# Attention scores of two tiles in one step, grouped by kind of matmul, and one ring of four PSUM banks for scores and transposes

## The chip, the cores and the metric

One core of one Trainium2 chip runs the whole program. The metric is the device time of one execution in microseconds, lower is better. TensorE (PE) does the matmuls, VectorE (DVE) and ScalarE (ACT) the elementwise work, SyncE (SP) issues most transfers, GpSimd (POOL) does little.

## The reference

One layer of an encoder, 2048 tokens of width 1024, on a grid of 32 rows by 64 columns. After an adaptive layer norm one input projection feeds two branches: a gated linear recurrence in both directions (HGRN, 8 heads of 128) and a neighbourhood attention (16 heads of 64, a window of 8 rows by 16 columns, clamped at the grid's edge, with a bias table). Both are gated, concatenated, projected by `w_out`, added to the input and normalised. The change touches the attention alone:

```
# _neighbourhood_attention, per grid row r, queries in 4 blocks of 16 columns, keys of 32 columns per block
s = jnp.einsum('bhjqd,bhrjcd->bhjqrc', q_row, k_blk).astype(jnp.float32) * scale
bias = jnp.take(col_bias, row_off, axis=1).transpose(0, 2, 3, 1, 4)
s = jnp.where(col_mask[:, :, None, :], s + bias[None], -jnp.inf)
p = jax.nn.softmax(s.reshape(B, H, nqb, NA_KC, KR * NA_SPAN), axis=-1)
o = jnp.einsum('bhjqrc,bhrjcd->bhjqd', p, v_blk)
...
y_na = o_na * jax.nn.silu(g_n)
```

## The kernel before, in words

**Stages.** The start and the first half of the attention (to about 560 us, with 8 head pairs over the first 8 grid rows), the recurrence (to about 1779 us), the second half of the attention (1779 to 2392 us, 8 head pairs over the other 24 rows), the output projection. A head pair is `w` in the first half, `u` in the second.

**A tile** is one block of 128 queries (8 grid rows, called a row group R, by 16 columns, number j) of two heads. A head pair has 4 tiles (R = 0) in the first half and 12 (R = 1, 2, 3 with j = 0 to 3) in the second. Keys of a tile are `nr` rows of 32 columns: 352, 480 or 384 in all. For one tile:

- `scores` has PE make two score banks (one per head): a product with the rounded keys, all 128 partitions high (KA and KB, L981), and added onto it one with the small remainder of the keys, 64 partitions high (KL, L984; "half-height"). The rounding is that of the fp32r type.
- Softmax, per head: DVE adds the bias, negates and takes the minimum (`shifted`, L993), ACT exponentiates and sums (`powers`, L998), DVE takes the reciprocal (L1002) and multiplies (`shares`, L1003).
- `turned` has PE transpose the shares in blocks of 128 (L1025) into PSUM; DVE and ACT copy them to SBUF (L1029, L1031).
- `sums` multiplies them with the values (L1044): per tile 16 matmuls of 128 columns by 64 (12 for R = 3). When a row group's four tiles are done, DVE multiplies by the gate into `yv` (L1054).

**The step.** `natten_woven` goes through the tiles one at a time. Step i issues the scores of tile i, then the sums of tile i-2, then hands over to the dense matmuls, then the transposes of tile i-1 (`turn(pipe, 2)`), then dense matmuls again, and then the tasks listed for step i.

**Dense matmuls** (L259, `pj`) are the projections of the next head pair's queries, keys, values and gates, three per group and eight groups per result in the second half; `weave` issues them between the pieces of a step. Each `yield x` of the step says how much: total / steps times x, in units of 0.68 per group. In the second half `steps` is 24 with two yields of 1 for each of the 12 tiles, which makes about six matmuls at each yield. Weights are split into a rounded part and a remainder by ACT and DVE (`wh`, `wl`, L758, L759).

**Tasks** prepare what comes next (`prep_now`, `prep_next`): `k` splits a piece of the next head pair's keys (rounded part on ACT, L922; remainder on DVE, L924), `q` the queries (L907, L908 on ACT, L909, L910 on DVE), `gate` makes the gate (L937, L317, L318, L319, L939), `table` loads a bias table, `v` the values. In the second half there is one set of KA, KB and KL: keys of the next head pair are written, piece by piece, over rows that this head pair's later tiles no longer read, and a piece waits for the matmuls that read it last. In the first half there are two sets.

**The order.** The program fixes PE's order by hand (as the code is written); DVE's, ACT's and SP's order within the attention comes from a scheduler, in which the softmax and the copies have priority (`tc.high_priority`). Each engine runs its instructions in the order given.

**PSUM.** The attention's eight banks: two for scores (`sc`), two for transposes (`pt`), two for sums (`po`), and two outside this table for dense results.

## Time and profile before

| | us |
|---|---|
| median of three runs | 2708.0 |
| lowest and highest run | 2706.22 and 2708.6 |
| span of the profiled execution | 2706.9 |
| second half of the attention | 1779 to 2392 |
| one head pair of it (five alike) | 67.1 |

The profile is of one execution, and its span is the profiled execution's own time. How to read it: the first line of the page gives each engine's busy time, its share of the span and its number of instructions (x). PE is TensorE's matmuls, PEld its weight loads, which run beside them. In rows of the timeline the columns are start in us, duration, engine, line of the kernel, operation, output <- inputs by the program's names, partitions x elements, number of instructions in the row (x), and in square brackets the idle time of the engine before it with what ended it. A pipelined matmul's duration is longer than the distance to the next one's start, so distances of starts are what PE spends. In group rows the numbers behind the bar are busy us in total, mean ns of one, and the idle time ahead of them. In rows of windows, each engine's busy time is followed by the number of its instructions, then the granted TensorE clock (1.00 is full), the DMA engines' share and GB/s.

### The profile page before, as it was taken

To read this page: it belongs to the slowest core of one execution; us is meant where nothing else is said; L and a number is where in the kernel's file an instruction comes from. 1 tells how busy PE (TensorE), PEld (TensorE's weight loads), DVE (VectorE), ACT (ScalarE), POOL (GpSimd) and SP (SyncE) were. 2 spreads that over 40 slices of the span, in tenths; PEclk is the share of its full clock that TensorE was granted. 3 is DMA by queue.
4 is the path that set the end of the run, shared out by engine and by line. 5 is a ranking of instruction groups with operands and counts; after the bars stand their busy time and mean duration, and the time that the engine had idled before them with its cause. 6 is when DMAs were issued, how large, how long until landed. Compare 5 with 4: busy or idle time off the path is not lost.

```text
span 2706.9 us, 46031 instructions
## 1 busy us (share of the span) xinstructions
PE 2612.5 (97%) x17328; PEld 2156.8 (80%) x17328; DVE 1766.4 (65%) x4351; ACT 1425.5 (53%) x2808; POOL 105.3 (4%) x142
## 2 busy tenths in 40 slices
PE   4999999989999999999999999989999999899998
PEld 3888888878888888888888888887777776678887
DVE  5445445477777778878777786455777777648443
ACT  4534444366666666666666666344666666431110
POOL 0000000000000000000000000000000000032221
PEclk8999999999999999999999999999999999999999
DMA  6566454212111126212222112354445445344331
GB/s 240 153 189 161 126 171 148 103 50 75 63 63 63 59 75 223 82 36 75 75 75 75 63 61 94 100 158 124 122 126 130 126 132 137 105 138 139 98 93 55
DMA packets 226559, 296.45 MB, mean 110 GB/s; under 512 B 28456, under 2 KB 117288, under 8 KB 226217
## 3 DMA queue, kind: packets, MB, share of 16 engines
q1 hardware_dynamic: 226337, 293.52, 35.3%
q8 instruction: 136, 2.23, 0.3%
q14 instruction: 86, 0.70, 0.1%
HBM read 218.24 MB, written 66.99 MB: 105 GB/s over the span
## 4 chain that ended last, share of the span: by engine, by line
PE 71%; DMA 2%; DVE 2%; ACT 1%; SPq 1%; issue 0%; DVEq 0%; ACTq 0%
PE pj L259 38%; PE ps L1384 4%; PE ps L1385 4%; PE ps L1386 4%; PE ps L1044 3%; PE ps L1025 3%; PE pj L272 2%; PE ps L458 2%; PE ps L450 1%; PE ps L981 1%; PE ps L984 1%; PE ps L525 1%; PE ps L497 1%; PE ps L549 1%; PE ps L551 1%; PE ps L623 1%
## 5 line engine op out<-in xcount | busy, mean ns | idle before, releaser
L259 PE MATMUL pj<-h,wh 128*128 128x512 f32 x4016 | 1289.1, 402 | 11.4 <-ACT h L224 6.2
L259 PEld LDWEIGHTS pj<-h,wh 128*128 128x128 f32 x4016 | 727.9, 189 | 173.3 <-issue 21.3
L259 PE MATMUL pj<-h,wl 128*128 128x512 f32 x2008 | 788.6, 393 | 0.1
L259 PEld LDWEIGHTS pj<-h,wl 128*128 128x128 f32 x2008 | 378.2, 188 | 83.2 <-DVE wl L759 0.5
L998 ACT ACTIVATE pbuf<-pbuf,mx 128x480 f32<-128x480 f32 (+2 forms) x256 | 164.3, 643 | 174.8 <-DVE mx L993 174.0
L993 DVE CUSTOM_DVE_ANT_1 pbuf<-ps,bias 128x480 f32<-128x480 f32 (+2 forms) x256 | 144.0, 595 | 134.9 <-PE ps L984 121.4
L272 PE MATMUL pj<-wh,h 128*128 128x256 f32 x1024 | 195.7, 288 | 0.3 <-ACT e L732 0.3
L272 PEld LDWEIGHTS pj<-wh,h 128*128 128x128 f32 x1024 | 163.6, 193 | 4.2 <-issue 2.5
L249 ACT ACTIVATE wh<-wr 128x512 fp32r<-128x512 f32 x192 | 120.2, 626 | 82.2 <-PE pj L259 69.3
L250 DVE TENSOR_TENSOR wl<-wr,wh 128x512 fp32r<-128x512 f32 x192 | 131.7, 686 | 46.6 <-ACT wh L249 45.6
L272 PE MATMUL pj<-wl,h 128*128 128x256 f32 x512 | 145.6, 284 | 0.0
L1031 ACT ACTIVATE pt<-ps 128x512 f32<-128x512 f32 (+1 forms) x128 | 69.1, 540 | 132.3 <-PE ps L1025 132.0
L1029 DVE COPY pt<-ps 128x512 f32<-128x512 f32 (+1 forms) x128 | 79.3, 619 | 84.2 <-PE ps L1025 83.2
L1044 PE MATMUL ps<-pt,V 128*64 128x128 f32 x1408 | 108.3, 285 | 16.1 <-ACT pt L1031 7.8
L444 DVE TENSOR_TENSOR de<-e,de 128x512 f32<-128x512 f32 x64 | 44.3, 692 | 118.9 <-ACT de L443 118.9
L1025 PE MATMUL ps<-ident,pbuf 128*128 128x128 f32 x896 | 119.2, 273 | 1.5 <-DVE pbuf L1003 1.5
L1025 PEld LDWEIGHTS ps<-ident,pbuf 128*128 128x128 f32 x896 | 105.6, 141 | 17.4 <-issue 2.3
L1044 PEld LDWEIGHTS ps<-pt,V 128*64 128x64 f32 x1408 | 76.1, 138 | 44.5 <-issue 20.7
L1003 DVE TENSOR_SCALAR pbuf<-pbuf,mx 128x480 f32<-128x480 f32 (+2 forms) x256 | 108.2, 437 | 5.1
L1360 ACT ACTIVATE yh<-yr 128x512 fp32r<-128x512 f32 x52 | 32.7, 629 | 130.9 <-PE ps L1385 113.9
L1433 DVE TENSOR_TENSOR vt<-ps,gt 128x512 f32<-128x512 f32 x24 | 16.5, 692 | 127.6 <-PE ps L1386 127.6
L272 PEld LDWEIGHTS pj<-wl,h 128*128 128x128 f32 x512 | 99.0, 193 | 0.8 <-issue 0.5
(266 smaller groups left out, 4634.3 us busy)
## 6 DMA issues: line engine op xcount, KB each, us to landing
wr<-in_w_in SPq DMA_DIRECT2D x276, 256.0 KB
V<-nv SPq DMA_DIRECT2D x256, 64.0 KB
yr<-yq SPq DMA_DIRECT2D x64, 256.0 KB
bias<-tint SPq DMA_DIRECT2D x24, 480.0 KB
x<-in_x SPq DMA_DIRECT2D x32, 256.0 KB
ada<-in_ada_w SPq DMA_DIRECT2D x16, 512.0 KB
wr<-in_w_v SPq DMA_DIRECT2D x32, 256.0 KB
nv<-vt SPq DMA_DIRECT2D x32, 256.0 KB
```

The source lines that it names most:

```text
L249: act.activation(hi, raw, AF.Copy)
L250: dve.tensor_tensor(lo, raw, hi, op=ALU.subtract)
L259: pe.matmul(pz, a, b, start=(k == 0 and n == 0), stop=(k == KT - 1 and n == 2))
L272: pe.matmul(pzs[tp][:, i * 256:(i + 1) * 256], a, b, start=(k == 0 and n == 0 and i == 0), stop=(k == KT - 1 and n == 2), skip_group_check ...
L993: return dve.tensor_tensor_reduce(s[:, 0:nk].rearrange("p (r c) -> p r c", c=32), sc[:, 0:nk].rearrange("p (r c) -> p r c", c=32), bt[:, 0 ...
L998: act.activation(s[:, 0:nk], s[:, 0:nk], AF.Exp, scale=-1.0, bias=mx[:, 0:1], accum_out=mx[:, 1:2])
L1003: dve.tensor_scalar(s[:, 0:nk], s[:, 0:nk], mx[:, 2:3], 1.0, op0=ALU.mult, op1=ALU.mult)
L1025: pe.transpose(ptp[:, c * P:(c + 1) * P], s[:, c * P:(c + 1) * P], ident)
L1044: pe.matmul(self.po[R][hs_, j * P:(j + 1) * P], self.st.V[c0 + c][:, j * P + hh * 64:j * P + hh * 64 + 64], pts[hh][:, c * P:(c + 1) * P], ...
L1384: pe.matmul(pz, yh[:, kk], wh, start=first, stop=False)
L1385: pe.matmul(pz, yh[:, kk], wl, start=False, stop=False)
L1386: pe.matmul(pz, yl[:, kk], wh, start=False, stop=last)
```

## The change

`scores` takes two tiles of one row group at once. It issues their four key matmuls, then their four half-height ones; the softmax is a method of its own and is called once for each tile. A step of `natten_woven` now covers two tiles: scores of both, `sums` of both tiles of the step before (32 matmuls in a block, 24 for R = 3), dense matmuls (0.8), transposes of this step's first tile, dense matmuls (1.8), transposes of this step's second tile, tasks of the first, dense matmuls (1.4), tasks of the second. So the transposes of a tile come in the step of its scores; before, they came one step (one tile) later. `turn` is gone. Score and transpose banks are one ring of four (`sp`) instead of two and two; the start keeps two and two in its own PSUM phase (`SPS`). The last head pair of the first half spreads its dense matmuls over 8 instead of 10. The computed values are the same.

```diff
-        def scores(self, R, j):
+        def scores(self, R, js):
+
             k0, nr = TILE[R]
-            bt = self.st.table(KIND[R], j)
             nk = nr * 32
-            scs = [ps("sc"), ps("sc")]
-            qs = [z[:, j * P:(j + 1) * P] for z in self.st.Q[R]]
             keys = keysets[self.p % len(keysets)]
...
-            for hh in range(2):
-                pe.matmul(scs[hh][:, 0:nk], qs[hh], kv(("KA", "KB")[hh]), start=True, stop=False, skip_group_check=True)
-            for hh in range(2):
-                hs_ = slice(hh * 64, hh * 64 + 64)
-                pe.matmul(scs[hh][:, 0:nk], qs[hh][hs_], kv("KL")[hs_], start=False, stop=True, skip_group_check=True)
+            for j in js:
+                bt = self.st.table(KIND[R], j)
+                scs = [ps("sc"), ps("sc")]
+                qs = [z[:, j * P:(j + 1) * P] for z in self.st.Q[R]]
+                tiles.append((j, bt, scs, qs))
+                for hh in range(2):
+                    pe.matmul(scs[hh][:, 0:nk], qs[hh], kv(("KA", "KB")[hh], j), start=True, stop=False, skip_group_check=True)
+            for j, bt, scs, qs in tiles:
+                for hh in range(2):
+                    hs_ = slice(hh * 64, hh * 64 + 64)
+                    pe.matmul(scs[hh][:, 0:nk], qs[hh][hs_], kv("KL", j)[hs_], start=False, stop=True, skip_group_check=True)
+            return [self.softmax(nr, bt, scs) for j, bt, scs, qs in tiles]
...
-        for i, (R, j) in enumerate(n.order):
-            pipe.append([n, R, j, n.scores(R, j)])
-            if len(pipe) > 2:
-                m, r, c, pts = pipe.pop(0)
-                m.sums(r, c, pts)
-            yield 1
-            turn(pipe, 2)
-            yield 1
+
+        def tasks(i):
             for f, *a in now.get(i, []) + later.get(i, []) + extra.get(i, []):
                 f(*a)
+
+        for i in range(0, len(n.order), 2):
+            R, js = n.order[i][0], [j for _, j in n.order[i:i + 2]]
+            ss = n.scores(R, js)
+            sums(pipe)
+            yield 0.8
+            p0 = n.turned(R, ss[0])
+            yield 1.8
+            p1 = n.turned(R, ss[1])
+            tasks(i)
+            pipe += [(n, R, js[0], p0), (n, R, js[1], p1)]
+            yield 1.4
+            tasks(i + 1)
...
-    NPS = {"sc": 2, "pt": 2, "po": 2}
+    SPS = {"sc": 2, "pt": 2, "po": 2}
+    NPS = ({"sp": 4, "po": 2}, {"sc": "sp", "pt": "sp"})
...
-                nxt, dense, total, steps = None, hgrn_dense(0, 0, feed=feed), HTOT, 10
+                nxt, dense, total, steps = None, hgrn_dense(0, 0, feed=feed), HTOT, 8
...
-    with psum_phase("n1", NPS), phase("n1", NB1, SM1), tc.manual_schedule(engines={mybir.EngineType.PE}):
+    with psum_phase("n1", *NPS), phase("n1", NB1, SM1), tc.manual_schedule(engines={mybir.EngineType.PE}):
```

Two places of the order show the change. The first is PE in the second half, head pair u = 2, at the last two tiles of R = 2. Before, the last tile but one: scores, sums of the tile two before it, six dense matmuls, then transposes of the tile before it (`pbuf` numbers name the shares' buffers; the sums' and dense matmuls' further rows are left out).

```order
L981 MATMUL ps_21145<-KA_3552_18657,Q_20498 128x480
L981 MATMUL ps_21146<-KB_3553_18658,Q_20499 128x480
L984 MATMUL ps_21145<-KL_3554_18659,Q_20498 128x480
L984 MATMUL ps_21146<-KL_3554_18659,Q_20499 128x480
L1044 MATMUL ps_21161<-pt_21121,V_20432 64x128
...
L259 MATMUL pj_21135<-h_10754,wh_20915 128x512
...
L1025 MATMUL ps_21184<-ident,pbuf_18651 128x128 x4
L1025 MATMUL ps_21191<-ident,pbuf_18653 128x128 x4
```

Now, the pair: both tiles' keys, both tiles' half-heights, 32 sums (the first is shown), three dense matmuls, and transposes of the pair's own first tile.

```order
L985 MATMUL ps_21163<-KA_3552_18661,Q_20516 128x480
L985 MATMUL ps_21164<-KB_3553_18662,Q_20517 128x480
L985 MATMUL ps_21167<-KA_3552_18661,Q_20516 128x480
L985 MATMUL ps_21168<-KB_3553_18662,Q_20517 128x480
L989 MATMUL ps_21163<-KL_3554_18663,Q_20516 128x480
...
L1053 MATMUL ps_21195<-pt_21094,V_20491 64x128
...
L259 MATMUL pj_21153<-h_10758,wh_20971 128x512
...
L1034 MATMUL ps_21215<-ident,pbuf_18659 128x128 x4
L1034 MATMUL ps_21222<-ident,pbuf_18651 128x128 x4
```

What moved: key and half-height matmuls stand in one block each, sums of two tiles in one, and the transposes read `pbuf_18659` and `pbuf_18651`, the shares of the scores issued just above (`ps_21163` and `ps_21164`), where before they read those of the tile before.

The second place is DVE at the same pair. Before, the last tile of R = 2 (the 128x1 rows store the minima; ISA is the shifted score): the pieces of the next head pair's keys and queries (L924, L909, L910) stand between the tile's shifted scores and its reciprocals.

```order
L993 ISA pbuf_18649,mx_21229<-ps_21223,bias_20737 128x480
L993 ISA mx_21229 128x1
L924 TENSOR_TENSOR KL_3554_18659<-bk_20953,KA_3552_18657 64x256
L993 ISA pbuf_18651,mx_21234<-ps_21224,bias_20737 128x480
...
L924 TENSOR_TENSOR KL_3554_18659<-e_21133,KB_3553_18658 64x256
L909 TENSOR_TENSOR Q_21284<-e_20864,Q_21284 64x512
L910 TENSOR_TENSOR Q_21285<-e_20864,Q_21285 64x512
L1002 RECIPROCAL mx_21229<-mx_21229 128x1
L1029 COPY pt_21258<-ps_21253 128x512
L1002 RECIPROCAL mx_21234<-mx_21234 128x1
L1003 TENSOR_SCALAR pbuf_18649<-pbuf_18649,mx_21229 128x480
```

Now, the pair of the last two tiles of R = 2, from its third shifted score on:

```order
L1002 ISA pbuf_18653,mx_21185<-ps_21167,bias_20753 128x480
...
L924 TENSOR_TENSOR KL_3554_18663<-bk_21012,KA_3552_18661 64x256
...
L1002 ISA pbuf_18655,mx_21190<-ps_21168,bias_20753 128x480
...
L924 TENSOR_TENSOR KL_3554_18663<-e_21151,KB_3553_18662 64x256
L909 TENSOR_TENSOR Q_21302<-e_20882,Q_21302 64x512
L910 TENSOR_TENSOR Q_21303<-e_20882,Q_21303 64x512
L1011 RECIPROCAL mx_21175<-mx_21175 128x1
L1011 RECIPROCAL mx_21180<-mx_21180 128x1
L1011 RECIPROCAL mx_21185<-mx_21185 128x1
L1011 RECIPROCAL mx_21190<-mx_21190 128x1
L1012 TENSOR_SCALAR pbuf_18659<-pbuf_18659,mx_21175 128x480
```

What moved: the same key and query pieces stand now ahead of the reciprocals and shares of both tiles of the pair, the first tile's too; before, the first of the two tiles had its shares (`pbuf_18655`, `pbuf_18647`) ahead of them.

## The prediction

> **What bounds the kernel now.** I read the page's busy shares and chain first, then the waits of PE in the second half of the attention, then the same stretch cut into windows of one head pair.

> ```profile
> span 2706.9 us, 46031 instructions
> PE 2612.5 (97%) x17328; PEld 2156.8 (80%) x17328; DVE 1766.4 (65%) x4351; ACT 1425.5 (53%) x2808; POOL 105.3 (4%) x142
> ...
> PE 71%; DMA 2%; DVE 2%; ACT 1%; SPq 1%; issue 0%; DVEq 0%; ACTq 0%
> ```

> PE is busy 97% of the span and is the chain: a microsecond in which PE waits is a microsecond of the kernel. DVE at 65% and ACT at 53% have room on the mean, which says nothing of the moment at which PE wants their result. Of 335 us in the second half, PE waits this long:

> ```profile
> PE ps L1044 <- DVE pt L1029: 2.0, 4, 0.5
> ...
> 1889.50:1956.60 67.10, 67.10 (x461) 51.58 (x459) 51.20 (x145) 43.51 (x98) 0.92 (x3) 1.00 0.46 123
> ...
> 2157.90:2225.00 67.10, 66.60 (x459) 51.33 (x458) 51.45 (x149) 43.41 (x98) 0.92 (x3) 1.00 0.49 129
> ```

> The windows (columns: length, busy PE, weight loads, DVE, ACT, POOL, granted clock, DMA share, GB/s) are the first and last of five head pairs, 67.1 us each, at a clock of 1.00. So two things can happen: PE does fewer or cheaper instructions (gain), or it begins to wait (loss). The program's matmuls stay the same in number; only their order changes.

> **What grouping saves.** This is PE's timeline over one tile, with the key matmuls of the tile before at 1991.04:

> ```profile
> 1991.04 0.39 PE L981 MATMUL ps<-KA,Q 128*128 128x480 f32 x1
> ...
> 1996.78 0.38 PE L981 MATMUL ps<-KA,Q 128*128 128x480 f32 x1
> 1997.00 0.38 PE L981 MATMUL ps<-KB,Q 128*128 128x480 f32 x1
> 1997.31 0.49 PE L984 MATMUL ps<-KL,Q 64*128 64x480 f32 x2
> 1997.73 0.88 PE L1044 MATMUL ps<-pt,V 128*64 128x128 f32 x12
> ...
> 1998.75 0.73 PE L259 MATMUL pj<-h,wh 128*128 128x512 f32 x2
> 1999.32 0.39 PE L259 MATMUL pj<-h,wl 128*128 128x512 f32 x1
> ...
> 2000.24 0.27 PE L1025 MATMUL ps<-ident,pbuf 128*128 128x128 f32 x1
> ```

> Starts are what counts. Key to key is 0.22, key to half-height 0.31 (0.09 more); two half-height matmuls to the sums take 0.42, where I take 0.22 for one step without a change, so 0.2 more; the sixteen sums take 1.02 to the first dense matmul, of which about 0.13 is the change in and out; the first two dense matmuls take 0.57 instead of 0.46 (0.11 more). That is 0.53 us of changes per tile, and one of two falls away per pair: 48 pairs in the second half by 0.53 are 25 us, 16 in the first by about 0.45 (narrower tiles) are 7. **Gross gain: 32 us**; zero if these gaps are work and not changes, no more than 32 since nothing else is left out.

> [...]

> **What it costs: the cover of the softmax.** Before, a tile's transposes come one step after its scores. The tile whose key matmul starts at 1991.04 is transposed at 2000.24, 9.2 us later (the transposes at 1994.51 are of the tile before it). In the changed order they come in the same step. Count from a pair's first key matmul: four keys and four half-heights end at 1.6 (3 x 0.22 + 0.31 + 3 x 0.21, sums at 1.60), 32 sums last about 1.9, then there are only three dense matmuls (0.8): **PE wants the first tile's shares at 4.3 us**, in the last pair of a head pair, where the sums are fewer, at 3.6, in the first pair, with six dense matmuls, at 4.5. Now what DVE does before that, in an undisturbed tile and in one that collides with the next head pair's key and query work:

> ```profile
> 1992.10 0.66 DVE L993 CUSTOM_DVE_ANT_1 pbuf<-ps,bias 128x480 f32<-128x480 f32 x1 [1.99 <-PE ps L984]
> ...
> 1992.68 0.65 DVE L993 CUSTOM_DVE_ANT_1 pbuf<-ps,bias 128x480 f32<-128x480 f32 x1
> ...
> 1993.62 0.16 DVE L1002 RECIPROCAL mx<-mx 128x1 f32<-128x1 f32 x1 [0.28 <-ACT pbuf L998]
> 1993.82 0.47 DVE L1003 TENSOR_SCALAR pbuf<-pbuf,mx 128x480 f32<-128x480 f32 x1
> ...
> 1997.83 0.66 DVE L993 CUSTOM_DVE_ANT_1 pbuf<-ps,bias 128x480 f32<-128x480 f32 x1 [1.06 <-PE ps L984]
> ...
> 1998.41 0.41 DVE L924 TENSOR_TENSOR KL<-bk,KA 64x256 fp32r<-64x256 f32 x1
> 1998.75 0.64 DVE L993 CUSTOM_DVE_ANT_1 pbuf<-ps,bias 128x480 f32<-128x480 f32 x1
> ...
> 1999.33 0.41 DVE L924 TENSOR_TENSOR KL<-e,KA 64x256 fp32r<-64x256 f32 x1
> ...
> 2000.56 0.68 DVE L909 TENSOR_TENSOR Q<-e,Q 64x512 fp32r<-64x512 f32 x1
> 2001.28 0.69 DVE L910 TENSOR_TENSOR Q<-e,Q 64x512 fp32r<-64x512 f32 x1
> 2002.00 0.16 DVE L1002 RECIPROCAL mx<-mx 128x1 f32<-128x1 f32 x1
> ...
> 2002.73 0.83 DVE L1003 TENSOR_SCALAR pbuf<-pbuf,mx 128x480 f32<-128x480 f32 x2
> ```

> The first shifted score starts 1.06 after the first key matmul; in a pair the half-heights come 0.44 later, so at 1.5. Undisturbed, the first share ends 2.2 after the first shifted score; collided, 5.3 after it. Both had 9.2 us. In a pair there are four shifted scores ahead instead of two, and in every second pair all key and query work of the next head pair as well, since it waits for the pair's last key matmuls and then stands ahead of the reciprocals in DVE's order. Prices: shifted score 0.58, the four key pieces 0.34 + 1.23 = 1.57, query pieces 0.72 each, reciprocal 0.08, share 0.47, and from these groups:

> ```profile
> L1054 DVE TENSOR_TENSOR yv<-ps,sg 128x128 f32<-128x128 f32 x48 | 10.8, 281 | 0.0
> ...
> L939 DVE TENSOR_TENSOR sg<-e,sg 128x512 f32<-128x512 f32 x8 | 5.5, 692 | 0.7 <-ACT sg L319 0.7
> ...
> L317 DVE TENSOR_SCALAR sg<-sg 128x512 f32<-128x512 f32 x12 | 5.0, 421 | 0.0
> ...
> L924 DVE TENSOR_TENSOR KL<-bk,KA 64x512 fp32r<-64x512 f32 x4 | 2.7, 678 | 0.0
> ```

> The six pairs of a head pair, by the order that the changed program gives DVE, with 0.1 us to hand over:
> - first: 1.5 + four shifted 2.32 + 0.42 (L317) + two reciprocals 0.16 + four yv about 0.86 + share 0.47 + 0.1 = 5.8, wanted at 4.5: **wait 1.3**
> - second: 1.5 + 2.32 + two key pieces of 512 1.38 + queries 1.44 + four reciprocals 0.32 + 0.47 + 0.1 = 7.5, wanted at 4.3: **3.2**
> - third: 1.5 + 2.32 + 0.16 + 0.47 + 0.1 = 4.55: **0.25**
> - fourth: as the second with key pieces of 1.57: 7.7: **3.4**
> - fifth: 384 columns, shorter shifted scores: in time, **0**
> - sixth: four shifted 1.9 + 1.57 + 1.44 + three reciprocals 0.24 + share 0.42, from 1.45, + 0.1 = 7.1, wanted at 3.6: 3.5, and the gate product (L939, 0.69) stands between the first and the second share, so the second half of the transposes waits some 0.7 more: **4.2**

> Sum 12.4 us of waiting per head pair. ACT gives nearly the same time for the collided pairs:

> ```profile
> 1997.20 0.42 ACT L922 ACTIVATE KA<-bk 64x256 fp32r<-64x256 f32 x1 [0.95 <-PE ps L981]
> ...
> 1998.69 0.63 ACT L907 ACTIVATE Q<-e 64x512 fp32r<-64x512 f32 x1
> ...
> 2000.00 0.70 ACT L998 ACTIVATE pbuf<-pbuf,mx 128x480 f32<-128x480 f32 x1
> ```

> From the first key piece to the first power are 2.8 us; in a pair that starts at 0.9, four powers by 0.69 end at 6.4, and the first share stands behind the fourth reciprocal. Speeding up one of the two engines would not remove the wait. Against 12.4 stand 6 x 0.53 = 3.2 saved and 0.4 of the old wait: **+8.8 us per head pair at full clock.** The ends: no wait at all, or, for a collided pair, what a collided tile takes today (5.3) with two more shifted scores (1.2) and two more powers (1.4), from 1.5 on: 9.4, which is a wait of 5.1. That would be 4 to 5 us more per head pair, nothing would be 12.4 less; I stay with the sums, since each entry has a row.

> **The clock.** PE of before stalls here and there, and after a stall it runs slowly:

> ```profile
> 1840.43 0.73 PE L259 MATMUL pj<-h,wh 128*128 128x512 f32 x2 [1.75 <-ACT wh L758]
> ...
> 1841.70:1845.00 3.30, 3.30 (x12) 2.61 (x11) 0.06 (x1) 0.00 (x0) 0.00 (x0) 0.50 0.57 142
> ...
> 2224.40:2296.70 72.30, 68.41 (x458) 52.63 (x457) 54.87 (x155) 45.55 (x100) 0.91 (x3) 0.98 0.49 135
> ```

> After a wait of 1.75 us, 3.3 us have a granted clock of 0.50: 1.65 us lost. Three waits per head pair (3.2, 3.4, 4.2) are longer than that one, so I add 3 x 1.65 = 4.95: **+13.75 us per head pair**, 67.1 to about 80.9. If stalls of that length only sometimes do it, the price lies between 0 and 4.95; I take the upper end, as the row is a shorter stall than these.

> [...]

> **Sum.** Five head pairs (u = 1 to 5) by 13.75: 69. The one after them (72.3 us today with a stall and a slow stretch at its end): 8.8 plus one slow stretch or so: 11, between 3 and 19. The first of the half is late today already for its bias table:

> ```profile
> 1799.08 0.66 DVE L993 CUSTOM_DVE_ANT_1 pbuf<-ps,bias 128x480 f32<-128x480 f32 x1 [5.65 <-DMA bias<-tint]
> ```

> There the second tile's transposes now stand in the same step as its scores and wait for that table: the 13.75 and some 3 more, 17 (9 to 25). The last head pair has no next one to prepare and collides with nothing: -3. First half: the changes saved (-7), against a shared bank that comes free late: there the four banks also take the transposed pieces of the input, which ACT evicts in this group, 0.77 us each (mean ns behind the busy time):

> ```profile
> L222 ACT ACTIVATE s<-ps,shift,scale 128x512 f32<-128x512 f32 x16 | 12.4, 774 | 12.5 <-PE ps L220 12.3
> ```

> The changed order has eight pairs there whose fourth key matmul takes such a bank: eight times somewhat under one eviction are about 5. And in one pair the transposes come behind the statistics of the next piece in DVE's order, for which I put as much as for the worst collided pair above with its slow stretch, 6: 5 + 6 - 7 = 4 (from -7, if no wait appears, to +12). The end: -1. Together 69 + 11 + 17 - 3 + 4 - 1 = 97: **2706.9 + 97 = 2804 us.** The span lies 1.1 us below the median of the runs, within their scatter, so the sum is taken as it is.

> **The rivals.**
> 1. *Only the changes are saved; faster.* Place: the reciprocals and shares of a pair's first tile on DVE. If they are through 4.3 us after the pair's first key matmul, no pair waits, and the kernel takes 2707 - 32 = 2675. For it speaks that DVE is idle a quarter of the time; against it that the order of DVE has the four key and two query pieces ahead of the reciprocals. It decides below 4.3 us; with a mean wait of 0.6 us per pair the gain is gone. 8%.
> 2. *Waits without slow clock.* The waits as worked out, no slow stretch: 97 less 20 stretches by 1.65 = 64: 2771. For it: many gaps of PE of about 1 us are followed by a full clock. 20%.
> 3. *The banks become the wait.* Transposes and scores share four banks; if each pair's key matmuls waited for one copy (about 0.7 us) and the transposes for nothing, 64 x 0.7 - 32 = 13: 2720. Against it: in the second half some eight dense matmuls stand behind the second transposes. 4%.
> 4. *No change in time.* Waits of half the size in the three collided pairs and no slow clock make gain and loss equal: 2708. 4%.

> Forecast: 64%. **The numbers:** 2804 is the likeliest. Without the slow clock and with waits 20% smaller (2.5 us by six) the time is 2756; waits 20% larger with all slow stretches give 2819, and the upper ends for the first half and the first head pair another 16: 2835. The range 2750 to 2835 leaves out rivals 1, 3 and 4. A measurement can tell about 0.2% (5 us) from no change: faster 0.08, same 0.04, slower 0.88.

> **What would show it.** Right: in the PE waits of the changed kernel, transposes that wait for DVE's shares are the largest group, three waits of over 3 us in each head pair, 80 us per head pair, and a granted clock near 0.9 there instead of 1.00; keys, half-heights and sums in one block each, 3 us less of changes per head pair. Wrong: transposes that start without a wait some 4.3 us after the pair's first key matmul, or score matmuls that wait for copies. The clock term is wrong if the windows keep 1.00.

## The result, and the profile after

| | before | changed |
|---|---|---|
| median, us | 2708.3 | 2796.9 |
| lowest and highest run | 2706.2 and 2709.9 | 2794.2 and 2799.0 |
| span of the profiled execution | 2706.9 | 2792.2 |

The changed kernel is slower: ratio 1.0326, 95% interval 1.0311 to 1.034. The forecast was 2804, with a range from 2750 to 2835. First the top of the changed kernel's page (busy time, share of the span, instructions of each engine) and its chain:

```profile
span 2792.2 us, 46302 instructions
## 1 busy us (share of the span) xinstructions
PE 2613.3 (94%) x17328; PEld 2176.8 (78%) x17328; DVE 1748.6 (63%) x4351; ACT 1424.6 (51%) x2808; POOL 106.7 (4%) x142
...
PE 66%; DVE 6%; DMA 3%; ACT 2%; issue 1%; SPq 0%; DVEq 0%; ACTq 0%
```

PE does as many matmuls and is busy as long as before, though the grouping saves changes between kinds of matmul (3.1 us per head pair, measured in experiment 6). There, with the same matmuls and the same grouping but no waits for shares in u = 1 to 5, PE is busy for 63.49 us in a head pair at a granted clock of 1.00; here it is busy for 70.12 us in the head pair u = 2, whose mean clock is 0.92. A slower clock uses up what the grouping saves. The chain has 6% of DVE where it had 2%. This is the list of PE's waits in the second half (line of the waiting matmul, what it waited for, us in total, times, longest):

```profile
PE ps L1034 <- DVE pbuf L1012: 58.5, 24, 3.7
```

This is over 420 us, from 1880 us on; the same five head pairs (u = 1 to 5) had 2.0 us of waits before. Of the 58.5, 55.9 belong to these five, 11.2 per head pair. Transposes (L1034) wait for shares (L1012), as the forecast had it. One such place on PE's timeline, the fourth pair of a head pair (second tiles of R = 2, the place that the order rows show):

```profile
2021.03 0.38 PE L985 MATMUL ps<-KA,Q 128*128 128x480 f32 x1
2021.25 0.39 PE L985 MATMUL ps<-KB,Q 128*128 128x480 f32 x1
2021.47 0.38 PE L985 MATMUL ps<-KA,Q 128*128 128x480 f32 x1
2021.69 0.38 PE L985 MATMUL ps<-KB,Q 128*128 128x480 f32 x1
2022.01 0.71 PE L989 MATMUL ps<-KL,Q 64*128 64x480 f32 x4
...
2024.54 0.73 PE L259 MATMUL pj<-h,wh 128*128 128x512 f32 x2
2025.11 0.40 PE L259 MATMUL pj<-h,wl 128*128 128x512 f32 x1
2028.71 1.07 PE L1034 MATMUL ps<-ident,pbuf 128*128 128x128 f32 x8 [3.20 <-DVE pbuf L1012]
2029.53 0.93 PE L259 MATMUL pj<-h,wh 128*128 128x512 f32 x2
2030.26 0.63 PE L259 MATMUL pj<-h,wl 128*128 128x512 f32 x1
```

The transposes are due at 2025.3 (three dense matmuls behind 2024.54), 4.3 us after the first key matmul, and start at 2028.71, 7.7 us after it. What holds them is on DVE's timeline of the same stretch:

```profile
2022.53 0.66 DVE L1002 CUSTOM_DVE_ANT_1 pbuf<-ps,bias 128x480 f32<-128x480 f32 x1 [3.10 <-PE ps L989]
...
2024.27 0.41 DVE L924 TENSOR_TENSOR KL<-bk,KA 64x256 fp32r<-64x256 f32 x1
2024.61 0.41 DVE L924 TENSOR_TENSOR KL<-e,KA 64x256 fp32r<-64x256 f32 x1
2024.94 0.64 DVE L1002 CUSTOM_DVE_ANT_1 pbuf<-ps,bias 128x480 f32<-128x480 f32 x1
...
2027.13 0.69 DVE L910 TENSOR_TENSOR Q<-e,Q 64x512 fp32r<-64x512 f32 x1
2027.85 0.34 DVE L1011 RECIPROCAL mx<-mx 128x1 f32<-128x1 f32 x4
2028.11 1.59 DVE L1012 TENSOR_SCALAR pbuf<-pbuf,mx 128x480 f32<-128x480 f32 x4
```

DVE hardly rests from 2022.53 to 2029.6: four shifted scores, four key pieces, two query pieces, four reciprocals, then the first share. With all four reciprocals ahead of the first share, as DVE's order has them, the share could not have been much earlier, since ACT's last power of the pair ends at 2027.5:

```profile
2026.75 0.68 ACT L1007 ACTIVATE pbuf<-pbuf,mx 128x480 f32<-128x480 f32 x1
2027.33 0.19 ACT L1007 ACTIVATION_READ_ACCUMULATOR pbuf<-pbuf,mx 128x1 f32 x1
```

And the clock, in windows right behind the waits of 3.06 and 3.20 us of the head pair u = 2 and in one behind a wait of 0.93 us (the number in front of the DMA share is the granted clock):

```profile
2002.46:2005.90 3.44, 3.44 (x11) 2.71 (x10) 2.06 (x4) 1.63 (x3) 0.00 (x0) 0.51 0.07 23
...
2029.53:2032.90 3.37, 3.37 (x12) 2.65 (x11) 2.06 (x4) 1.63 (x3) 0.00 (x0) 0.55 0.36 122
...
1988.20:1991.00 2.80, 2.80 (x16) 2.34 (x15) 2.04 (x5) 1.52 (x4) 0.00 (x0) 1.00 0.44 153
```

Where the 85.3 us between the two spans lie, by the first key matmul of each head pair on the two timelines:

| stretch | before, us | changed, us | difference |
|---|---|---|---|
| start to the second half's first key matmul | 1779.2 | 1778.2 | -1.0 |
| u = 0 | 110.3 | 123.6 | +13.3 |
| u = 1 to 5 together | 334.9 | 400.3 | +65.4 |
| u = 6 | 72.3 | 91.3 | +19.0 |
| u = 7 and the rest | 410.2 | 398.8 | -11.4 |

### The profile page after: what moved, and what is told of

Same layout as the page of the kernel before. It is cut to its first block, busy times and chain, and to the rows that moved or that the text cites. A ratio compares the mean times of both kernels' runs of the same rounds, so it can differ in the third digit from the quotient of the medians.

```text
span 2792.2 us, 46302 instructions
## 1 busy us (share of the span) xinstructions
PE 2613.3 (94%) x17328; PEld 2176.8 (78%) x17328; DVE 1748.6 (63%) x4351; ACT 1424.6 (51%) x2808; POOL 106.7 (4%) x142
## 4 chain that ended last, share of the span: by engine, by line
PE 66%; DVE 6%; DMA 3%; ACT 2%; issue 1%; SPq 0%; DVEq 0%; ACTq 0%
PE pj L259 36%; PE ps L1396 4%; PE ps L1395 4%; PE ps L1397 4%; PE ps L1034 3%; PE pj L272 2%; PE ps L458 2%; DVE pbuf L1002 2%; PE ps L985 1%; PE ps L450 1%; PE ps L525 1%; PE ps L497 1%; PE ps L1053 1%; PE ps L549 1%; DVE KL L924 1%
## 5 line engine op out<-in xcount | busy, mean ns | idle before, releaser
L259 PE MATMUL pj<-h,wh 128*128 128x512 f32 x4016 | 1299.0, 405 | 9.5 <-ACT h L224 6.1
L259 PEld LDWEIGHTS pj<-h,wh 128*128 128x128 f32 x4016 | 743.8, 192 | 170.2 <-issue 12.0
L259 PE MATMUL pj<-h,wl 128*128 128x512 f32 x2008 | 794.9, 396 | 0.4 <-DVE wl L759 0.4
L259 PEld LDWEIGHTS pj<-h,wl 128*128 128x128 f32 x2008 | 383.3, 191 | 85.0 <-DVE wl L759 0.9
L1002 DVE CUSTOM_DVE_ANT_1 pbuf<-ps,bias 128x480 f32<-128x480 f32 (+2 forms) x256 | 141.2, 594 | 127.1 <-PE ps L989 104.3
L1034 PE MATMUL ps<-ident,pbuf 128*128 128x128 f32 x896 | 129.1, 286 | 95.0 <-DVE pbuf L1012 78.8
L1034 PEld LDWEIGHTS ps<-ident,pbuf 128*128 128x128 f32 x896 | 107.8, 147 | 121.5 <-issue 108.4
L732 ACT ACTIVATE e<-pj 128x512 f32<-128x512 f32 x100 | 59.5, 596 | 150.4 <-PE pj L259 145.8
L1012 DVE TENSOR_SCALAR pbuf<-pbuf,mx 128x480 f32<-128x480 f32 (+2 forms) x256 | 103.9, 435 | 2.5
L1053 PE MATMUL ps<-pt,V 128*64 128x128 f32 x1408 | 96.7, 278 | 0.0
```

Of the source, the lines that this page charges most:

```text
L259: pe.matmul(pz, a, b, start=(k == 0 and n == 0), stop=(k == KT - 1 and n == 2))
L1002: return dve.tensor_tensor_reduce(s[:, 0:nk].rearrange("p (r c) -> p r c", c=32), sc[:, 0:nk].rearrange("p (r c) -> p r c", c=32), bt[:, 0 ...
L1012: dve.tensor_scalar(s[:, 0:nk], s[:, 0:nk], mx[:, 2:3], 1.0, op0=ALU.mult, op1=ALU.mult)
L1034: pe.transpose(ptp[:, c * P:(c + 1) * P], s[:, c * P:(c + 1) * P], ident)
L1053: pe.matmul(self.po[R][hs_, j * P:(j + 1) * P], self.st.V[c0 + c][:, j * P + hh * 64:j * P + hh * 64 + 64], pts[hh][:, c * P:(c + 1) * P], ...
```

## The experiments

All times are medians, all ratios are to the kernel before, run on the same chip, with the 95% interval. "Period" is the length of a head pair for u = 1 to 5.

**1. More dense matmuls ahead of the first transposes.** If the wait is for want of cover, cover removes it.

```diff
+            ya, yb, yc = (2.8, 0.6, 0.6) if st.half and nxt else (0.8, 1.8, 1.4)
             sums(pipe)
-            yield 0.8
+            yield ya
             p0 = n.turned(R, ss[0])
-            yield 1.8
+            yield yb
             p1 = n.turned(R, ss[1])
...
-            yield 1.4
+            yield yc
```

> In the second half, for the head pairs that have a next one, the dense matmuls of a step are shared out 2.8, 0.6, 0.6 instead of 0.8, 1.8, 1.4, so some 2.8 us more of them stand ahead of the first tile's transposes. Grouping and ring stay. Theory (cover of the softmax too short, and the slow clock that follows the waits): the three long waits per head pair (3.1, 3.2, 3.7 us) shrink to under 1 us each, the granted clock goes back to 1.00, a head pair takes 65 to 66 us instead of 80, and the kernel 2700 us (2690 to 2715). Rival (the ring of four banks, or the grouping itself, makes the wait): the time stays at 2780 to 2795.

Measured: 2706.2 us, ratio 0.9993 (0.9984 to 1.0002), period 66.4 us, in this head pair at full clock:

```profile
1956.91:2023.26 66.35, 63.81 (x457) 51.06 (x456) 49.27 (x148) 43.03 (x97) 0.92 (x3) 1.00 0.46 127
```

The whole loss goes, though the grouping and the ring stay. The waits of a head pair that are left are 0.3, 0.9 + 0.4 and 0.8 us. The shares come no sooner: in the second pair, DVE's order is that of the changed kernel (key and query pieces, four reciprocals, then the first share), and the transposes start 7.5 us after the first key matmul, as they do there. But now PE has dense matmuls to do until then:

```profile
1968.04 0.38 PE L985 MATMUL ps<-KA,Q 128*128 128x480 f32 x1
...
1975.59 1.07 PE L1034 MATMUL ps<-ident,pbuf 128*128 128x128 f32 x8 [0.34 <-DVE pbuf L1012]
```

The rival falls.

**2. The clock by itself.** PE is given work without use while it waits.

```diff
...
+                for _ in range(fill if hh == 0 else 0):
+                    pe.matmul(ptp[:, 0:512], ones, hts[1, 7, 0], start=True, stop=True, skip_group_check=True)
...
-            p0 = n.turned(R, ss[0])
+            p0 = n.turned(R, ss[0], 12 if st.half and st.p < 6 and i % 4 == 2 else 0)
```

> The changed kernel with 12 matmuls of 128x512 without use (some 2.8 us) ahead of the first tile's transposes of every second pair, for u = 0 to 5 of the second half: PE is busy while it waits, but the transposes come no sooner. Theory (a slow clock of 3.3 us after each wait of over 1.75 us, 1.65 us lost each): 18 slow stretches go, the granted clock there goes to 1.00, 2792 - 30 = 2763 us. [...]

Measured: 2774.1 us, ratio 1.0246 (1.023 to 1.0261), period 75.6 instead of 80.05 us. On PE's timeline the work without use fills the second pair's wait, and the window of that whole head pair has a granted clock of 1.00, where the changed kernel's had 0.92:

```profile
1995.89 2.97 PE L1034 MATMUL ps<-h,ones 128*128 128x512 f32 x12
1999.03 1.10 PE L1036 MATMUL ps<-ident,pbuf 128*128 128x128 f32 x8 [0.16 <-DVE pbuf L1012]
...
1979.31:2054.93 75.62, 72.78 (x494) 57.61 (x493) 49.43 (x148) 43.21 (x97) 0.92 (x3) 1.00 0.42 113
```

The transposes still start 7.5 us after the pair's first key matmul (1991.57), so the wait is as long as it was; only the idleness is gone. That is worth 4.45 us per head pair, 1.5 per wait on the mean. The total fell by 23 us, less than the 30 expected: five head pairs give 22, and u = 0, which was filled as well, nothing that can be seen (123.6 us in the changed kernel, 124.3 here). More matmuls, less time, for u = 1 to 5.

**3. The score matmuls not grouped.** The two loops over the tiles become one:

```diff
-            for j, bt, scs, qs in tiles:
                 for hh in range(2):
                     hs_ = slice(hh * 64, hh * 64 + 64)
```

> The changed kernel with the score matmuls of the two tiles not grouped: two keys and two half-heights of the first tile, then of the second. All else stays, grouped sums too. Theory (where PE waits for DVE, the saved changes between kinds of matmul are worth nothing; the first tile's scores now come 0.44 us sooner, and so does the end of the wait): four waiting pairs gain 0.4 us or more, the others lose 0.3: 2778 to 2792 us. Rival (grouping is worth its 0.3 us in each of the 64 pairs, whatever waits): 2792 + 18 = 2810 us.

Measured: 2784.5 us, ratio 1.0279 (1.0261 to 1.0296), period 78.6: faster than with the grouping. PE's waits over the five head pairs, here and (second line) in the changed kernel:

```profile
PE ps L1033 <- DVE mx L1010: 39.3, 15, 3.4
...
PE ps L1034 <- DVE pbuf L1012: 55.9, 23, 3.7
```

The scheduler also put DVE's work in another order here (in the second pair the first share stands ahead of the last three reciprocals), so not all of the shorter waits, 2.2, 2.3 and 3.4 us, comes from scores that start sooner, and the total does not separate the two. Two pairs of u = 2 are clean. The first has the same order on DVE in both kernels; its transposes start 5.2 instead of 5.7 us after the first key matmul, and it is 0.4 us shorter. The fifth has no wait in either; it is 0.4 us longer (10.6 against 10.2). So grouping the scores gains where PE does not wait, and costs where it waits for shares.

**4. The ring alone**, in the kernel of before.

```diff
-    NPS = {"sc": 2, "pt": 2, "po": 2}
+    SPS = {"sc": 2, "pt": 2, "po": 2}
+    NPS = ({"sp": 4, "po": 2}, {"sc": "sp", "pt": "sp"})
```

> The kernel of before with the ring of four banks for scores and transposes alone: one tile a step, in the old order. Theory (the banks are not what costs): 2707 us, within 4. Rival (the ring makes score matmuls wait for copies): 0.3 to 0.7 us per tile in 128 tiles, 2745 us or more.

Measured: 2708.0 us, ratio 0.9995 (0.9985 to 1.0004), and the same 2.0 us of PE's waits in the second half as before. The ring costs nothing when the order is the old one.

**5. Key remainders left out.** This changes one of the two engines that the prediction took to be late together.

```diff
-                dve.tensor_tensor(keys["KL"][x, o], raw[x], z[x, o], op=ALU.subtract)
+                if not (self.half and self.p):
+                    dve.tensor_tensor(keys["KL"][x, o], raw[x], z[x, o], op=ALU.subtract)
```

> The changed kernel without the remainders of the keys (KL, DVE) for u = 1 to 7 of the second half: the products take the remainder of u = 0, so the output is not the reference's; all matmuls stay. Theory (the key work of DVE that stands ahead of the reciprocals is 1.4 to 1.6 us of each long wait): the waits of 3.1, 3.2 and 3.7 us shrink to 1.5 to 2 us, some slow stretches go with them, the kernel takes 2740 to 2765 us. Rival (ACT's powers set the end just as DVE does, so DVE's key work is worth 0.3 us each): 2785 us or more.

Measured: 2746.9 us, ratio 1.0137 (1.0123 to 1.0151). Waits of PE over four head pairs and two windows of 3.4 us behind waits, of 1.71 and 2.20 us:

```profile
PE ps L1035 <- DVE mx L1012: 15.6, 8, 2.2
PE ps L1035 <- DVE pbuf L1013: 10.6, 8, 1.7
...
1990.40:1993.80 3.40, 3.40 (x20) 2.94 (x20) 2.88 (x7) 1.64 (x4) 0.00 (x0) 1.00 0.20 63
...
2037.30:2040.70 3.40, 3.40 (x12) 2.77 (x11) 3.10 (x9) 2.80 (x8) 0.00 (x0) 0.52 0.60 125
```

Waits of 3.1, 3.2 and 3.7 us are now 1.7, 1.7 and 2.2, each about 1.5 us shorter, as the first theory had it, and with them all but some of the slow stretches go (a clock of 0.98 or 1.00 for whole head pairs). So ACT did not keep the wait where it was. But the order of DVE changed with it: without the key pieces the scheduler puts the first share behind the second reciprocal, not the fourth, so it no longer waits for ACT's last two powers:

```profile
2013.44 0.22 DVE L1012 RECIPROCAL mx<-mx 128x1 f32<-128x1 f32 x2
2013.64 0.85 DVE L1013 TENSOR_SCALAR pbuf<-pbuf,mx 128x480 f32<-128x480 f32 x2
```

How much would have been left with the old order, the run cannot say.

**6. Shares of dense work set pair by pair.** Experiment 1 with its left-over waits covered:

```diff
+            ya, yb, yc = ((2.8, 0.6, 0.6), (3.2, 0.6, 0.6), (2.4, 0.6, 0.6), (3.2, 0.6, 0.4), (2.0, 0.6, 0.6), (3.6, 0.7, 0.3))[i // 2] if st.half and nxt else (0.8, 1.8, 1.4)
```

> As the run with 2.8, 0.6, 0.6, but with the shares of the dense matmuls set pair by pair by the waits that were left there (0.3, 0.9 + 0.4 and 0.8 us in a head pair): 2.8, 3.2, 2.4, 3.2, 2.0, 3.6 ahead of the first transposes of the six pairs. Theory (the cover alone decides, and the grouping is worth about 3.3 us per head pair where nothing waits): 63.5 to 64.5 us per head pair, the kernel 2691 us (2682 to 2700). Rival (the grouping is worth nothing, the waits go elsewhere): 2703 to 2712 us.

Measured: 2692.6 us, ratio 0.9932 (0.992 to 0.9945): **faster than both kernels**. Period 64.1. A head pair, and PE's waits over four of them:

```profile
1952.66:2016.77 64.11, 63.49 (x459) 51.32 (x458) 49.28 (x150) 42.80 (x98) 0.92 (x3) 1.00 0.49 134
...
PE ps L985 <- ACT pt L1040: 2.5, 4, 0.6
```

PE's busy time is 63.49 against 66.60 before: 3.1 us of changes saved per head pair, the 6 x 0.53 = 3.2 that the prediction worked out. In u = 1 to 5 no transposes wait for shares any more; the one wait left is for a bank of the ring, 0.6 us, now that dense work between the last transposes and the next key matmuls is short.

**7. The first half alone.** The old step in the second half, the pairs in the first.

```diff
+        if st.half:
+            for i, (R, j) in enumerate(n.order):
+                pipe.append([n, R, j, n.scores(R, [j])[0]])
+                if len(pipe) > 2:
+                    m, r, c, pts = pipe.pop(0)
+                    m.sums(r, c, pts)
+                yield 1
+                turn(pipe, 2)
+                yield 1
+                tasks(i)
+            return
...
```

> The changed kernel with the old step (one tile, transposes one tile later) in the second half: what is left of the change is the first half's pairs and the ring. Theory from the trace of the changed kernel (the second half begins 1.0 us sooner than before, saved changes and new waits nearly cancel there): 2707 us, within 4 of the kernel before. Rival (the prediction's sum for the first half, or more of the loss than the trace shows comes from there): 2712 us or more.

Measured: 2708.0 us, ratio 0.9994 (0.9986 to 1.0003). The first half's part of the change is nothing that can be told from zero; the loss is in the second half.

**8 and 9. Transposes one pair later.** First as a list of tiles that are transposed in the next step, six buffers for the scores:

```diff
+            if st.half:
+                prev = late[:]
+                late[:] = [(n, R, j, s) for j, s in zip(js, ss)]
...
             yield 0.8
-            p0 = n.turned(R, ss[0])
+            pipe += [(m, r, c, m.turned(r, s)) for m, r, c, s in prev[:1]]
             yield 1.8
-            p1 = n.turned(R, ss[1])
+            pipe += [(m, r, c, m.turned(r, s)) for m, r, c, s in prev[1:]]
```

> The changed kernel with the transposes of the second half put one pair later (as before the change, when they came one tile later), the shares of dense matmuls as in the change (0.8, 1.8, 1.4), six score buffers instead of five. Grouping and ring stay. Theory (the transposes' place is the whole loss): no wait for shares in u = 1 to 5, a clock of 1.00, 63.4 us per head pair, the kernel 2686 us (2678 to 2700). Rival (key matmuls then wait for banks, or the scores for buffers): 66 us and more per head pair, 2705 us or more.

Measured: 2853.3 us, ratio 1.0533 (1.0519 to 1.0548), slower than the change. PE's waits over four head pairs:

```profile
PE ps L1034 <- DVE pbuf L1012: 61.0, 12, 5.5
PE ps L1034 <- DVE mx L1011: 11.9, 12, 1.2
```

The edit did not do what it was meant to. With six buffers and four per pair, the third and fourth scores of a pair go into buffers that the pair before still had to have transposed. In program order the scores were written first, so those transposes read the later pair's shares and waited for them, up to 5.5 us. As a test of the theory it says nothing. Next, the second tile's softmax stands behind the first transposes of the pair before:

```diff
-            return [self.softmax(nr, bt, scs) for j, bt, scs, qs in tiles]
+            return [lambda bt=bt, scs=scs: self.softmax(nr, bt, scs) for j, bt, scs, qs in tiles]
...
+            s0 = ss[0]()
...
             yield 0.8
-            p0 = n.turned(R, ss[0])
+            pipe += [(m, r, c, m.turned(r, s)) for m, r, c, s in prev[:1]]
+            if st.half:
+                late[:] = [(n, R, js[0], s0), (n, R, js[1], ss[1]())]
             yield 1.8
...
```

> The intent of the run with late transposes, without its fault: there the third and fourth scores of a pair were written over buffers whose transposes still had to come, so half of the transposes read the next pair's shares and waited for them. Here the second tile's softmax comes behind the transposes of the pair before; shares of dense matmuls as in the change (0.8, 1.8, 1.4), six buffers. Theory (the transposes' place is the loss): no long wait for shares in u = 1 to 5, clock 1.00, 63.4 to 65 us per head pair, the kernel 2680 to 2700 us. Rival (banks or buffers then make PE wait): 66 us and more per head pair, 2705 us or more.

Measured: 2697.2 us, ratio 0.9957 (0.9943 to 0.997), period 65.0 in the undisturbed head pairs. Over three of them PE waits no longer for shares:

```profile
PE pj L259 <- DVE wl L759: 1.9, 3, 0.6
```

The change's own shares of dense work (0.8, 1.8, 1.4) are kept here, and so are the grouping and the ring. Besides the place of the transposes, the place of the second tile's softmax and the number of buffers differ, and DVE's order with them, so this run alone would not single out the place. With experiment 1, where DVE's order up to the first share stayed, it shows from a second side that the loss is the short time between scores and transposes. The run is 4.6 us behind experiment 6; its trace has a wait of 10.9 us for ACT at the first output matmuls, which that one has not.

## Why the prediction was right, and where its terms were off

The terms of a head pair, as predicted and as measured:

| term, us per head pair | predicted | measured | from |
|---|---|---|---|
| waits of the six pairs | 1.3, 3.2, 0.25, 3.4, 0, 4.2 | 0.9, 3.1, 0.1, 3.2, 0, 3.7 to 4.1 | PE's gaps, u = 1 to 5 |
| changes saved | 3.2 | 3.1 | busy PE, experiment 6 against before |
| slow clock | 4.95 | 4.45 | experiment 2 |
| head pair against before | +13.75 | +13.1 | 400.3 and 334.9 over five |

The measured terms (11.2 of waits, 3.1 saved, 0.4 of the old wait, 4.45 of clock) add up to 12.2; where the last 0.9 us lies was not separated.

- *Cover.* Shown: transposes due at 4.3 us after the first key matmul start at 7.7 (7.7 was forecast for this pair). Experiments 1, 6 and 9 take the wait away by more cover, in two ways.
- *Key and query work ahead of the reciprocals.* Shown for the key work: without it each long wait is about 1.5 us shorter. That speeding up one engine alone would not help, as the prediction said beside ACT's rows, did not hold: it held for the order given, but the order moved.
- *The clock.* The forecast had a slow stretch of 3.3 us behind each of the three long waits. In u = 1 to 5 there are 15 such waits. Nine are followed by 3.4 us at half clock, three by 6.8 us (from 1920.63, 2053.75 and 2292.69 on, about 1 us before the wait's end), and three (3.20, 3.07 and 3.21 us, ending at 1949.85, 2082.87 and 2188.85) by a full clock. One window behind a wait without a slow stretch, and one of the long slow stretches:

```profile
1949.90:1953.30 3.40, 3.40 (x20) 2.94 (x21) 2.74 (x6) 1.64 (x3) 0.00 (x0) 1.00 0.45 142
...
2053.80:2060.50 6.70, 5.80 (x16) 4.51 (x17) 4.07 (x13) 2.36 (x6) 0.00 (x0) 0.50 0.62 140
```

  That the price per head pair, 4.45, came close to 4.95 is in part luck: the longer stretches stand in for the missing ones.
- *Borders.* Their sum was right by luck; its parts were not. For u = 6, 11 (3 to 19) was forecast and 19.0 came; for the last head pair and the end, -3 and -1, and -11.4 came; together 7 forecast, 7.6 measured. At the end of u = 6 the last pair's transposes wait 10.3 us, since DVE's reciprocals stand behind splits of the output weights, which wait for ACT:

```profile
2376.82 0.22 DVE L1011 RECIPROCAL mx<-mx 128x1 f32<-128x1 f32 x2
2380.61 0.69 DVE L1356 TENSOR_TENSOR wo<-wr,wo 128x512 fp32r<-128x512 f32 x1 [3.56 <-ACT wo L1355]
2381.21 0.15 DVE L1011 RECIPROCAL mx<-mx 128x1 f32<-128x1 f32 x1
```

  Before, PE had waits of 3.6 and 4.4 us in u = 7:

```profile
2301.30 0.43 PE L1044 MATMUL ps<-pt,V 128*64 128x128 f32 x2 [3.60 <-DVE pt L1029]
...
2306.14 0.48 PE L1044 MATMUL ps<-pt,V 128*64 128x128 f32 x1 [4.41 <-ACT pt L1031]
```

  Now one of 4.6 is left there. The prediction read u = 7 as undisturbed, counted no wait that leaves it, and did not see that the output weights' splits would come ahead of u = 6's last reciprocals. What else makes up the -11.4 was not separated.
- *First head pair.* 17 (9 to 25) forecast, 13.3 measured: in range. Its longest waits are 7.8 (4.5 before), 4.8 and 2.6 us; which of its terms was taken too high, no run separates.
- *First half.* +4 forecast, -1.0 in the trace, nothing in experiment 7. The waits that were forecast are there, for the bank and for one pair's reciprocals:

```profile
PE ps L1034 <- DVE mx L1011: 4.9, 1, 4.9
PE ps L985 <- ACT s L222: 4.5, 7, 1.2
```

  They came to 9.4 us, and 5.5 us at a clock of 0.50 behind the longer one add 2.75: 12.2 where 11 was taken. On the other side the sum left out a wait of the kernel before, 2.1 us with 3.4 us at a clock of 0.50 behind it, which the changed kernel does not have:

```profile
294.48 0.73 PE L259 MATMUL pj<-h,wh 128*128 128x512 f32 x2 [2.11 <-ACT wh L784]
...
295.40:298.80 3.40, 3.40 (x9) 2.48 (x8) 0.96 (x2) 0.07 (x1) 0.00 (x0) 0.50 0.72 243
```

  That is 3.8 us. With the 7 us that the sum counts as saved, it leaves about +1.4 where -1.0 came; the 7 were not measured by themselves.
- *The rivals.* "Only the changes are saved" decides at the cover, as said, and experiment 6 is that case brought about: 2692.6, not 2675. There u = 1 to 5 gain 15.6 us, while u = 0, u = 6 and what follows together are only 2.8 us shorter than before, and up to the start of u = 7 PE still has a wait of 4.1 us for shares and one of 5.3 us for a transfer. "The banks become the wait" is not seen in u = 1 to 5 of the changed kernel nor in experiment 4, except as the 0.6 us of experiment 6. In u = 6 and at the start of u = 7 it is: there score matmuls (L985) wait for copies of transposes, the sign that the forecast gave for being wrong, but only 9.3 us in all.

```profile
PE ps L985 <- ACT pt L1040: 4.7, 2, 2.4
PE ps L985 <- DVE pt L1038: 4.6, 1, 4.6
```

  "Waits without slow clock" is close to what experiment 2 built: 2774 against the 2771 given.

Had only the total been compared, the errors of single terms would not have been seen: u = 0, u = 1 to 5 and the first half came out 3.7, 3.6 and 5 us lower than forecast, u = 6 came out 8 higher, the last head pair and the end 7.4 lower.

## What to carry to other kernels

A regrouping that saves work on the engine that bounds a kernel has two sides: what it saves, and how long a result has from its request to its use. Count that second time in the new order before anything else, with all that stands ahead of the result on the engines that make it. Here 3.1 us per head pair were to be had, and moving the use from 9.2 to 4.3 us after the request cost five times as much (11.2 of waits and 4.45 of slow clock). With 3.4 to 4.7 us more of independent work ahead of the use in the three late pairs, as in experiment 6, the gain is there.

## What the runs showed of the hardware

A wait of PE can cost more than its length, since a slow clock can follow it. In the changed kernel 12 of the 15 long waits of u = 1 to 5 (3.06 to 3.73 us) were followed by 3.4 or 6.8 us at a granted clock of about 0.50, and three (3.07 to 3.21 us) by a clock of 1.00. In experiment 5, 1.71 us was not followed by a slow clock (1.00), 2.20 us was in one head pair (0.52) and not in the next (1.00 over the whole head pair); in the kernel before, 1.75 us was (0.50). So the length alone does not decide.

Useless matmuls in the wait kept the clock up in experiment 2: with 12 of them in each of three waits, a head pair had a clock of 1.00 instead of 0.92 and was 4.45 us shorter.
